# ScalarE in written order during the mLSTM outputs, own buffers for the decays' exponentials, and outputs that follow the states without a stop

## The chip, the cores and the metric

The kernel runs on one core of a Trainium2 chip. The metric is the device time of one execution in microseconds (us). Each engine of the core (TensorE for matmuls, VectorE, ScalarE, GpSimd, and SyncE, which here issues nearly all DMAs) works through its own list of instructions in the order that was fixed when the program was built, and waits on semaphores for the others. In the rows TensorE is PE (PEld its weight loads), VectorE is DVE, ScalarE is ACT, GpSimd is POOL, SyncE is SP.

## What is computed

Two layers of a hybrid backbone over 1024 latent tokens and 256 context tokens, width 1024. In each layer the tokens are normalised and modulated, and one input projection feeds three groups of heads:

```python
aq, ak, av, mq, mk, mv, mo, mg, pp = split(h @ w_in)
att  = softmax attention of 8 query heads on 2 key/value heads (aq, ak normalised and rotated)
ml   = bidirectional chunkwise mLSTM of (mq, mk, mv), gates from mg, read out through sigmoid(mo)
pool = centred means of pp over windows 2, 4, 8, 16, times a small matrix per group
x = x + g1 * (concat(att, ml, pool) @ w_out)
x = x + g2 * swiglu(norm(x))
```

The mLSTM of one direction runs over chunks of 128 tokens, for four heads of 64:

```python
b = cumsum(lf);  dmat = where(tril, b[:, None] - b[None, :] + li[None, :], -inf)
m_t = max(b + m, max(dmat));  w = exp(b + m - m_t)
s = (q @ k.T) * exp(dmat - m_t)              # the decays' exponentials
h = (w * (C @ q) + s @ v) / max(|den|, exp(-m_t))
C = a * C + v.T @ (wk * k)                   # the state, chunk after chunk
```

The second layer computes outputs for the latent tokens alone (8 chunks instead of 10).

## The kernel before

Python code writes the instructions of all engines in one sequence. A scheduler then fixes the order on each engine: it takes what is ready in its own estimate of times, the earlier written first, and gives out the buffers of each pool as it goes. An order that the code wants to keep is added as a dependency without a semaphore from one instruction to the next of the same engine; `InRow` (L87 to L105) does that for VectorE while a switch is on, and before the change that switch is on in one place, at the start of the feed-forward part (L1767 to L1794).

The in-projection of a layer runs TensorE as a row of GEMMs over one 128-column tile of `w_in` each (`gemm_tm` L796, `gemm_fm` L809), every one in blocks of 512 tokens (256 for the context), into PSUM banks of which this stage has 8. The work around the GEMMs is written as Python generators in the list `threads`; one call of `pump` lets every generator take one step. A block of 512 tokens gives two turns, one in the middle and one at its end, a block of 256 gives one. The step that a generator takes in a turn stands, in written order, between the halves of the GEMM or behind the block's eviction by ScalarE. `drain` takes turns until a generator, or all, have ended, with no GEMM between the turns.

- `ml_states` (L922) computes the states: 18 units of chunk and direction; a unit is a front (matmul `pk`, DVE `kw`, ACT and POOL `kh`) and a back (matmul `pu`, DVE `C`, snapshots into `X`, whose memory holds `qml`, `kml`, `vau` and `snap` in this stage). It takes 2 + 18 turns, and one in which it ends.
- `ml_outputs(z)` (L972) runs two generators, for the even and the odd chunks. One chunk (`ml_chunk`) takes 7 turns: 1 the loads of `sgc` and `mrow` (SP); 2 the matmuls `pst` and the first direction's decays; 3 the second direction's decays and `pxi`; 4 and 5 the numerators (matmul `pi`, eight DVE instructions each, then the square on ACT and its reduction); 6 the root; 7 the gains; and behind the seventh, in the turn of the next chunk's loads, `oh` (ACT, DVE) and its store to `mld`. In `decay_` (L996) a bank `pm` receives the exponents, ACT takes four exponentials into the tile `E`, DVE multiplies `E` by the scores, ACT rounds to `Ah`, POOL subtracts the rounding.
- `c_qk` and `c_q` (L1086, L1116) hold a query or key block in `q` and `sqq` for some four turns (ACT evicts, DVE and POOL rotate, ACT rounds, SP stores); a key block holds a third buffer `r`. `pool_tile` (L1182) forms the window sums on POOL in `bA`, `bB`, and uses `pm` and `ph`. `ada_fill` adds one small product for the layer's modulation per block, in the first layer only.

`E`, `q`, `sqq`, `r`, `pm`, `ph`, and in earlier parts of the stage `t`, `sq`, `vf`, `kw` and others, are all tiles of one pool of 2 KiB buffers, `f2k`, with 8 of them in this stage. Before the change `drain(stg)` stands behind the GEMM of `O_MQ + P`: the states that are left then run without a GEMM beside them, and the outputs are spawned behind them. Then come the GEMMs `O_PP`, `O_AK`, `O_AQ`, `O_PP + P`, three more `O_AQ`, `O_AV`, and a last `drain()`: 40 turns in the first layer, 34 in the second.

The attention stage follows in `phase("s")`: SP first issues the transposes of `mld` into `mixT[:, 4:6]` (the same memory as `h1`, which the last GEMM reads), the load of `pld`, and four loads `X <- xs` into the memory that the mLSTM used; then each of the 64 (first layer 68) units runs `Sp` (PE), its maximum `mx` (DVE), the exponential `pf` (ACT), `phl` (ACT, POOL), a transposing DMA `pT <- phl`, and `pv` (PE). The first filling matmuls of that stage (`pwo`) read `mixT[:, 4:8]`.

Of the kernel before, what the change touches and what calls it, by code (L numbers as in the profile page):

```python
# [9 lines left out]
F32 = mybir.dt.float32  # L10
# [8 lines left out]
P = 128  # L19
# [62 lines left out]
def hybrid_kernel(ctx: ExitStack, tc: tile.TileContext, I, out, dbg=None):  # L82
    nc = tc.nc
    order = mybir.DependencyInfo(mybir.DependencyClass.NoSync, mybir.DependencyReason.DATA)
    row = {"on": False, "last": None}

    class InRow:  # L87

        def __init__(self, e):
            self.e = e  # L90

        def __getattr__(self, name):
            f = getattr(self.e, name)

            def call(*a, **k):
                b = f(*a, **k)  # L96
                if row["on"]:
                    if row["last"] is not None:
                        tc.add_manual_dep(b.ins, row["last"].name, order, reason="written order")
                    row["last"] = b.ins  # L100
                return b
            return call

    def in_row(on):
        row.update(on=on, last=None)  # L105

    V = InRow(nc.vector)
    S, G, TE, DMA = nc.scalar, nc.gpsimd, nc.tensor, nc.sync
    MUL, ADD, SUB, MAX, MIN = ALU.mult, ALU.add, ALU.subtract, ALU.max, ALU.min
    dbg = dbg or {}  # L110

# [4 lines left out]


    cur = {}
    F2K = {"g": 8, "s": 6}
    PFB, PHB, PTB = 2, 3, 5  # L120

    def phase(kind):
# [29 lines left out]
    def pt_(shape, dt, tag, bufs=1, name=None):  # L152
        return cur["w"].tile(list(shape), dt, tag=tag, name=name or tag, bufs=bufs)

    def f2k(shape=(P, 512), dt=F32, name="f2k"):
        return pt_(shape, dt, "f2k", F2K[cur["kind"]], name)

# [44 lines left out]
    threads = []  # L202

    def spawn(gen):
        threads.append(gen)
        return gen
# [20 lines left out]
    def drain(g=None):  # L227
        while (g in threads) if g is not None else threads:
            if g is None:
                pump()  # L230
            else:
                try:
                    next(g)
                except StopIteration:
                    threads.remove(g)
# [531 lines left out]
    for l in range(DEPTH):  # L767
        last = l == DEPTH - 1
# [203 lines left out]
        def ml_outputs(z):  # L972
            for c in range(z, nto, 2):
                yield from ml_chunk(c, z)

        def ml_chunk(c, z):
# [19 lines left out]
            def decay_(d):  # L996
                pm = bank("pm")
                mm(pm.rearrange("p (h t) -> p h t", h=4), idb, mskb[:, d].unsqueeze(1).to_broadcast([P, 4, P]), start=True, stop=False)
                mm(pm, one3, mrow[d], start=False, stop=True)
                E = f2k((P, 4, P), F32, "E")  # L1000
                for i, h in enumerate(HO):
                    r = d * 64 + c * 4 + h
                    act(E[:, i], pm[:, i * P:(i + 1) * P], AF.Exp, bias=tmq[:, 0, r:r + 1])
                Ev = E.rearrange("p h t -> p (h t)")
                for g in range(2):
                    stt(Ev[:, g * 256:(g + 1) * 256], pst[g][:, 0:256], 1.0 / 16, Ev[:, g * 256:(g + 1) * 256], MUL, MUL)
                Ah = pt_((P, 2, 4, P), F16, "Ah", 4)
                act(Ah[:, 0].rearrange("p h t -> p (h t)"), Ev)
                tt(Ah[:, 1], E, Ah[:, 0], SUB, G)
                Ahs.append(Ah)  # L1010
# [137 lines left out]
        def q_roots():  # L1148

            v = rq[:, :, :nto].rearrange("p a c h -> p a (c h)")  # L1150
            rstd(v[:, 0], nto * 8, v[:, 2], v[:, 1])
            V.tensor_scalar(v[:, 0], v[:, 1], 0.125 / 16, None, op0=MUL)
            V.tensor_scalar(v[:, 1], v[:, 1], -0.125 / 16, None, op0=MUL)
# [28 lines left out]
        def pool_tile(i, u):  # L1182
            S2, S4, S8, S16 = (1, 0), (1, 1), (2, 2), (4, 4)
            for (t0, n) in blks:
                ub = u[:, pcol(t0) - 8:pcol(t0) + n + 8]
                bA = pt_((P, 768), F32, "pb", 2, "bA")
                bB = pt_((P, 768), F32, "pb", 2, "bB")

                def win(o, s, sh, lo_, hi_, x):

                    tt(o[lo_:hi_, x:n + 16 - x], s[lo_:hi_, x - sh[0]:n + 16 - x - sh[0]],
                       s[lo_:hi_, x + sh[1]:n + 16 - x + sh[1]], ADD, G)

                if i == 0:
                    win(bA, ub, S2, 64, 128, 7)
                    win(bB, ub, S2, 0, 64, 8)
                    win(bB, bA, S4, 64, 128, 8)
                    fin = [bB, bB]
                else:
                    win(bA, ub, S2, 0, 128, 1)  # L1200
                    win(bB, bA, S4, 0, 128, 2)
                    yield
                    win(bA, bB, S8, 0, 128, 4)
                    win(bB, bA, S16, 64, 128, 8)
                    fin = [bA, bB]
                p = f2k((P, 512), F32, "pm")
                for g in range(2):
                    ps = slice(64 * g, 64 * g + 64)
                    f = fin[g][ps, 8:8 + n]
                    if t0 != 512:  # L1210
                        tt(f[:, 0:8], f[:, 0:8], edge[ps, i, 0:8], MUL, G)
                    if t0 != 0:
                        tt(f[:, n - 8:n], f[:, n - 8:n], edge[ps, i, 8:16], MUL, G)
                yield
                for g in ([0] if fin[0] is fin[1] else range(2)):
                    ps = slice(0, P) if fin[0] is fin[1] else slice(64 * g, 64 * g + 64)
                    stt(p[ps, :n], fin[g][ps, 8:8 + n], invw[ps, i:i + 1], ub[ps, 8:8 + n], MUL, SUB)
                yield
                pb = bank("ppool")
                mm(pb[:, :n], pw[:, i], p[:, :n], start=True, stop=True)  # L1220
                sc = ps16[:, l * 2 + i:l * 2 + i + 1]
                ph = f2k((P, 2, 512), F16, "ph")
                act(ph[:, 0, :n], pb[:, :n], scale=sc)
                stt(ph[:, 1, :n], pb[:, :n], sc, ph[:, 0, :n], MUL, SUB)
                DMA.dma_start(out=pld[:, i, :, t0:t0 + n], in_=ph[:, :, :n])
                yield
# [6 lines left out]
        for (t0, n) in BLOCKS:  # L1233
            if t0 in nx:
                drain(nx.pop(t0))
            for r in range(3):
                if t0 >= T and last and r == 2:
                    continue
                if l == 0 and t0 < T:
                    pb = pf0[r][t0 // 512]  # L1240
                else:
                    pb = bank("pfm")
# [42 lines left out]
        for i in range(2):  # L1285
            DMA.dma_start(out=cst[i], in_=I["t_cs"][:, i])
        gemm_fm(O_MQ + P, blks, c_ml(qml, 1, INV * 4))
        drain(stg)
        spawn(ml_outputs(0))
        spawn(ml_outputs(1))  # L1290
        def pool_gemm(i):
            u = pool_u()

# [15 lines left out]
        while next_is_ada() or pend:  # L1309
            ada_fill()  # L1310
        drain()
        q_roots()


# [449 lines left out]
        sg, Sg, Su = sgs[0], f0.pop("Sg"), f0.pop("Su")  # L1764
        f0.clear()
        act(sg[:, :NTq], Sg[:, :NTq], AF.Silu, scale=INV)
        in_row(True)  # L1767
        stt(sg[:, :NTq], Su[:, :NTq], 1.0 / SW, sg[:, :NTq], MUL, MUL)

        ho = h_ops()  # L1770
# [20 lines left out]
        for _ in ho:  # L1791
            pass
        drain()
        in_row(False)  # L1794
        for k in range(4):
            split2(h2[:, k, :, H1], scv[:, k], V)

# [270 lines left out]
```

## Time and profile before

| | us |
|---|---|
| median of 3 runs (2774.57 to 2776.82) | 2776.61 |
| profiled execution, its own time | 2780.47 |
| its span (first to last instruction) | 2778.7 |
| PE busy | 2564.7 (92%) |
| DVE busy | 1890.2 (68%) |
| ACT busy | 1387.1 (50%) |
| POOL busy | 1269.3 (46%) |

The profiled execution took 3.9 us longer than the median of the runs. A wait in the rows below stands in square brackets: how long the engine had been idle before the instruction, and which engine's instruction, on which tile, released it last. "x12" is a count of instructions that were merged into one line. The granted clock is the share of TensorE's full speed that the throttle gave; of its two levels, 1.2 and 2.4 GHz, the mean over a stretch is shown.

### The profile page before, as it was taken

The page shows a single profiled execution, that of the slowest core. Times are in us where ns is not written, and L with a number is a line of the kernel's source. Part 1 is how long each engine was busy: PE and PEld are TensorE (multiplying, and loading weights), DVE is VectorE, ACT ScalarE, POOL GpSimd, SP SyncE. Part 2 cuts the span into 40 slices and gives each one's busy share as a digit, 9 for nine tenths or more (in the row PEclk, how much of TensorE's full clock was granted, in tenths as well). Part 3 has the DMA queues.
Part 4 walks back from the last instruction along what each step waited for, and adds up shares of the span by engine and source line. Part 5 has one row for each costly group of instructions (what it writes and reads, how often), then busy time and mean ns, then how long its engine had stood idle before and what let it go on. Part 6 is the DMA issues. An engine that isn't in the chain of part 4 may idle for free. (4 is left out here: it accounts for less than half of the span.)

```text
span 2778.7 us, 53623 instructions
## 1 busy us (share of the span) xinstructions
PE 2564.7 (92%) x21403; PEld 1500.9 (54%) x21403; DVE 1890.2 (68%) x3233; ACT 1387.1 (50%) x2650; POOL 1269.3 (46%) x963
## 2 busy tenths in 40 slices
PE   7999989987899999999999998888878899999997
PEld 4875556655555555555554684455545344444444
DVE  5558867778766555656565557866777767667676
ACT  5345557766443434444344544466765444444453
POOL 1124446774334435444443213456763465555651
PEclk9999999999899999999999999999989899999999
DMA  9544489995132222223212222389993111111211
GB/s 301 144 123 113 126 203 184 190 177 121 57 92 81 87 84 84 86 82 92 61 46 78 69 55 57 115 185 182 191 174 102 46 53 54 62 61 54 61 53 76
DMA packets 631629, 296.21 MB, mean 107 GB/s; under 512 B 362888, under 2 KB 620756, under 8 KB 630868
## 3 DMA queue, kind: packets, MB, share of 16 engines
q1 hardware_dynamic: 631204, 292.73, 42.9%
q8 instruction: 167, 2.74, 0.4%
q14 instruction: 82, 0.67, 0.1%
q10 hardware_dynamic: 176, 0.07, 0.0%
HBM read 176.19 MB, written 20.87 MB: 71 GB/s over the span
## 5 line engine op out<-in xcount | busy, mean ns | idle before, releaser
L1960 PEld LDWEIGHTS <-hlp 128*128 128x128 f16 x5040 | 492.0, 98 | 602.7 <-issue 26.6
L1960 PE MATMUL Swb<-T,hlp 128*128 128x512 f16 x1920 | 445.6, 381 | 18.5 <-DVE sg L96 13.0
L195 POOL TENSOR_TENSOR phl<-pf,phl 128x1280 f16<-128x1280 f32 (+1 forms) x132 | 345.2, 2618 | 176.8 <-ACT phl L175 123.1
L96 DVE SCALAR_TENSOR_TENSOR hlp<-ws,hlp 128x512 f16<-128x512 f32 (+1 forms) x320 | 231.6, 732 | 112.0 <-ACT hlp L175 89.2
L175 ACT ACTIVATE hlp<-ws 128x512 f16<-128x512 f32 (+1 forms) x320 | 162.6, 518 | 210.7 <-PE Swb L1960 90.5
L175 ACT ACTIVATE pf<-Sp,mx,rq 128x1280 f32<-128x1280 f32 (+1 forms) x144 | 189.6, 1317 | 118.1 <-DVE mx L96 98.8
L96 DVE TENSOR_REDUCE mx<-Sp 128x1 f32<-128x1280 f32 (+1 forms) x132 | 195.0, 1477 | 63.4 <-PE Sp L1337 55.4
L1960 PE MATMUL Swb<-tq,hlp 128*128 128x512 f16 x960 | 223.4, 382 | 8.0 <-DVE hlp L96 4.6
L1960 PE MATMUL Swc<-T,hlp 128*128 128x512 f16 x960 | 227.2, 379 | 0.0
L1400 PE MATMUL pwo<-T,hl 128*128 128x512 f16 (+1 forms) x960 | 194.5, 354 | 34.0 <-DVE X L96 14.3
L492 PE MATMUL pfm<-T,hl 128*128 128x512 f16 (+1 forms) x1032 | 216.4, 363 | 4.2 <-ACT E L175 4.1
L1337 PE MATMUL Sp<-T 128*128 128x512 f16 (+1 forms) x800 | 169.3, 348 | 42.5 <-ACT pf L175 40.1
L96 DVE SCALAR_TENSOR_TENSOR hlp<-st,hlp 128x256 f16<-128x256 f32 (+1 forms) x201 | 149.0, 746 | 86.7 <-ACT hlp L175 73.8
L195 POOL TENSOR_TENSOR ws<-st 128x256 f32<-128x256 f32 (+1 forms) x97 | 104.4, 1083 | 170.1 <-DMA st<-in_w_ffn_down_dram 67.9
L175 ACT ACTIVATE T<-sg 128x512 f16<-128x512 f32 (+1 forms) x170 | 98.8, 599 | 165.0 <-POOL sg L195 96.3
L1972 PE MATMUL dx<-T,hlp 128*128 128x256 f16 x1440 | 177.3, 273 | 1.0 <-DVE hlp L96 1.0
L195 POOL TENSOR_TENSOR X<-X,T 128x512 f32<-128x512 f32 x80 | 114.1, 1427 | 139.8 <-DVE X L96 105.1
L1960 PE MATMUL Swa<-T,hlp 128*128 128x512 f16 x720 | 169.3, 380 | 0.0
L1972 PEld LDWEIGHTS <-hlp 128*128 128x128 f16 x1440 | 139.1, 100 | 33.1 <-issue 4.8
L1400 PEld LDWEIGHTS <-hl 128*128 128x128 f16 x960 | 97.7, 102 | 109.8 <-issue 40.8
L175 ACT ACTIVATE phl<-pf 128x1280 f16<-128x1280 f32 (+1 forms) x115 | 144.6, 1262 | 21.2 <-DMA pT<-phl 18.9
L195 POOL TENSOR_TENSOR sg<-sg,T 128x512 f32<-128x512 f32 x60 | 88.7, 1478 | 143.6 <-DVE T L96 143.2
(308 smaller groups left out, 4735.8 us busy)
## 6 DMA issues: line engine op xcount, KB each, us to landing
T<-in_w_ada_dram SPq DMA_DIRECT2D x48, 512.0 KB
rawa<-in_w_ada_dram SPq DMA_DIRECT2D x48, 512.0 KB
st<-in_w_in_dram SPq DMA_DIRECT2D x32, 512.0 KB
st<-in_w_out_dram SPq DMA_DIRECT2D x64, 256.0 KB
st<-in_w_ffn_gate_dram SPq DMA_DIRECT2D x32, 512.0 KB
st<-in_w_ffn_up_dram SPq DMA_DIRECT2D x30, 512.0 KB
st<-in_w_ffn_down_dram SPq DMA_DIRECT2D x30, 512.0 KB
xs<-X SPq DMA_DIRECT2D x4, 2048.0 KB
```

What stands on the lines that cost most here:

```text
L96: b = f(*a, **k)
L175: b = S.activation(o, i, f, **kw).ins
L195: (e or V).tensor_tensor(o, a, b, op=op)
L492: mm(o, w[:, a, k, :], h[:, k, b, t0:t0 + n], start=(k == 0 and j == 0), stop=(k == nk - 1 and j == 2))
L1337: mm(Sp[:, e * nk + b0:e * nk + b0 + m], ql, qkv[:, 4 + h // 4, a, k0 + b0:k0 + b0 + m], start=(a == 0), stop=(a == 1), skip_group_check=True)
L1400: mm(pb, w[:, a, k, :], mixT[:, k0 + k, b, t0:t0 + n], start=(k == 0 and j == 0), stop=(k == 3 and j == 2))
L1960: mm(o, w[:, a, k, :], B[:, b], start=(s in "172" and k == 0 and j == 0), stop=(k == kh(i) - 1 and j == 2), skip_group_check=True)
L1972: mm(dbank[i][:, r * 256:(r + 1) * 256], w[:, a, k, :], B[:, b], start=(first and k == 0 and j == 0), stop=(not first and k == kh(i) - 1 a ...
```

## The change

The order switch gets a name and exists for ScalarE too. It is turned on for ScalarE behind the GEMM of `O_MQ + P` and off behind the last `drain()` of the stage, in both layers. `E` no longer comes from `f2k` but from two buffers of its own; to make room, `f2k` has 7 buffers instead of 8 in this kind of stage (it is also the stage at the kernel's start, at the seam of the layers and at the end), and `bA`, `bB` shrink from 768 to the 528 columns that are used. `drain(stg)` goes: a small generator `outputs` waits in `threads` until the states have ended, and then spawns the two output generators, while the GEMMs go on.

```diff
-    row = {"on": False, "last": None}
+    rows = {}
     class InRow:
-        def __init__(self, e):
-            self.e = e
+        def __init__(self, e, name):
+            self.e, self.row = e, rows.setdefault(name, {"on": False, "last": None})
...
-    def in_row(on):
-        row.update(on=on, last=None)
-    V = InRow(nc.vector)
-    S, G, TE, DMA = nc.scalar, nc.gpsimd, nc.tensor, nc.sync
+    def in_row(on, *names):
+        for name in names:
+            rows[name].update(on=on, last=None)
+    V, S = InRow(nc.vector, "V"), InRow(nc.scalar, "S")
+    G, TE, DMA = nc.gpsimd, nc.tensor, nc.sync
...
-    F2K = {"g": 8, "s": 6}
+    F2K = {"g": 7, "s": 6}
+    INROW = ("S",)
...
-                E = f2k((P, 4, P), F32, "E")
+                E = pt_((P, 4, P), F32, "E", 2)
...
-                bA = pt_((P, 768), F32, "pb", 2, "bA")
-                bB = pt_((P, 768), F32, "pb", 2, "bB")
+                bA = pt_((P, 528), F32, "pb", 2, "bA")
+                bB = pt_((P, 528), F32, "pb", 2, "bB")
...
         gemm_fm(O_MQ + P, blks, c_ml(qml, 1, INV * 4))
-        drain(stg)
-        spawn(ml_outputs(0))
-        spawn(ml_outputs(1))
+        in_row(True, *INROW)
+
+        def outputs():
+            while stg in threads:
+                yield
+            spawn(ml_outputs(0))
+            spawn(ml_outputs(1))
+
+        spawn(outputs())
...
         drain()
+        in_row(False, *INROW)
         q_roots()
...
-        in_row(True)
+        in_row(True, "V")
...
-        in_row(False)
+        in_row(False, "V")
```

## Rows read from the trace of the kernel before

**Rows 1.** The busy time of each engine in the two stretches from the states' last units to the end of the in-projection (first layer, second layer): start and end, length, busy us (instructions) of PE, PEld, DVE, ACT and POOL, mean granted clock, DMA share, GB/s.

```profile
188.00:373.00 185.00, 176.23 (x1866) 109.92 (x1859) 148.15 (x422) 95.22 (x250) 72.13 (x77) 0.97 0.43 123
1657.00:1821.00 164.00, 145.89 (x1328) 81.49 (x1326) 131.20 (x351) 78.83 (x194) 61.82 (x60) 0.93 0.30 88
```

**Rows 2.** The same view for the two attention stages.

```profile
383.00:653.00 270.00, 234.23 (x2886) 155.80 (x2885) 197.47 (x248) 194.54 (x270) 186.12 (x82) 0.97 1.04 187
1829.00:2091.00 262.00, 214.28 (x2580) 136.58 (x2580) 186.20 (x217) 183.30 (x231) 179.13 (x75) 0.93 0.99 182
```

**Rows 3.** What PE waited for in the second layer's stretch: us in total, times, the longest.

```profile
PE pfm L492 <- ACT E L175: 4.1, 1, 4.1
PE pxi L1024 <- ACT E L175: 4.1, 3, 2.0
PE msq L1091 <- ACT sqq L175: 1.9, 1, 1.9
PE pm L998 <- ACT u L175: 1.1, 1, 1.1
```

**Rows 4.** The same in the first layer's stretch.

```profile
PE pm L998 <- DVE num L96: 2.0, 1, 2.0
PE pxi L1024 <- DVE prm L96: 1.6, 1, 1.6
PE ppool L1220 <- DVE dn L96: 1.2, 1, 1.2
```

**Rows 5.** PE in order of time where the states run out: the second layer, with one unit beside the GEMM ahead of it (first three rows), and the first layer (last two).

```profile
1653.83 0.39 PE L931 MATMUL pk<-id,X 128*128 128x128 f16 x4
1654.14 0.39 PE L945 MATMUL pu<-X,kh 128*64 128x65 f16 x12
1654.46 2.76 PE L492 MATMUL pfm<-T,hl 128*128 128x512 f16 x12
1657.06 0.39 PE L931 MATMUL pk<-id,X 128*128 128x128 f16 x4
...
1667.05 7.05 PE L492 MATMUL pfm<-T,hl 128*128 128x512 f16 x22
188.24 0.40 PE L931 MATMUL pk<-id,X 128*128 128x128 f16 x4
...
193.36 4.92 PE L492 MATMUL pfm<-T,hl 128*128 128x512 f16 x22
```

**Rows 6.** ACT, and below it PE, in order of time around the longest wait of the second layer's stretch.

```profile
1703.51 0.48 ACT L175 ACTIVATE q<-pfm,qkg 128x256 f32<-128x256 f32 x1
1710.46 1.14 ACT L175 ACTIVATE E<-pm,tmq 128x128 f32<-128x128 f32 x4 [5.26 <-POOL q L195]
```

```profile
1676.20 2.76 PE L492 MATMUL pfm<-T,hl 128*128 128x512 f16 x12
1711.65 4.44 PE L492 MATMUL pfm<-T,hl 128*128 128x512 f16 x12 [4.09 <-ACT E L175]
```

**Rows 7.** ACT, and below it PE, in order of time in two later places of that stretch.

```profile
1742.52 0.42 ACT L175 ACTIVATE oh<-T 128x256 f16<-128x256 f32 x1 [3.39 <-DVE T L96]
1779.38 0.63 ACT L175 ACTIVATE sqq<-q 128x512 f16<-128x512 f32 x1 [2.06 <-DVE q L96]
```

```profile
1681.10 2.33 PE L492 MATMUL pfm<-T,hl 128*128 128x512 f16 x10
1750.13 4.31 PE L492 MATMUL pfm<-T,hl 128*128 128x512 f16 x12
1787.79 3.82 PE L492 MATMUL pfm<-T,hl 128*128 128x512 f16 x10
```

**Rows 8.** VectorE's busy time in the 20 us in which the second layer's last chunk pair gets its outputs, for the instructions on the tile `num`, then for those on `T` (here the memory of the outputs `hs`).

```profile
1792.00:1812.00 20.00, 6.03 (x20) 1.00 0.64 205
```

```profile
1792.00:1812.00 20.00, 5.59 (x14) 1.00 0.64 205
```

**Rows 9.** Two groups of these VectorE instructions: duration in ns as min/median/max, first and last start.

```profile
L96 DVE TENSOR_TENSOR dn<-num,tmq x4: 153/162/1224, 1792.6 to 1799.3; 128x4 f32<-128x4 f32 x4
...
L96 DVE TENSOR_TENSOR T<-num,dn x4: 408/422/426, 1795.0 to 1802.3; 128x256 f32<-128x256 f32 x4
```

**Rows 10.** SP in order of time at the seams to the attention stage: second layer, then first layer.

```profile
1805.79 0.59 SPq L1321 DMA_DIRECT2D X<-xs  x1
1809.40 2.69 SPq L1083 DMA_DIRECT2D mld<-oh  x4
...
1818.82 4.30 SPq L1317 DMA_TRANSPOSE T<-mld  x2
...
1829.46 12.62 SPq L1366 DMA_TRANSPOSE pT<-phl  x3
```

```profile
372.14 8.59 SPq L1317 DMA_TRANSPOSE T<-mld  x2
```

**Rows 11.** PE at the same seams: the first filling matmuls of the attention stage, first layer, then second.

```profile
382.87 1.44 PE L1400 MATMUL pwo<-T,hl 128*128 128x512 f16 x3 [3.39 <-DMA T<-mld]
```

```profile
1825.82 1.46 PE L1400 MATMUL pwo<-T,hl 128*128 128x512 f16 x6 [2.38 <-DMA T<-mld]
```

**Rows 12.** What PE waited for in the first 84 us of the kernel: us in total, times, the longest.

```profile
PE pf L723 <- POOL T L195: 2.4, 4, 1.2
```

More of the change, by code (lines that the diff above doesn't have):

```diff
@@ L84, in hybrid_kernel @@
     order = mybir.DependencyInfo(mybir.DependencyClass.NoSync, mybir.DependencyReason.DATA)
-    row = {"on": False, "last": None}
+    rows = {}
     class InRow:
-        def __init__(self, e):
-            self.e = e
+        def __init__(self, e, name):
+            self.e, self.row = e, rows.setdefault(name, {"on": False, "last": None})
         def __getattr__(self, name):
-            f = getattr(self.e, name)
+            f, row = getattr(self.e, name), self.row
             def call(*a, **k):
```

## The prediction

> **What bounds the kernel now.** I read the busy table of the page first (PE 92% of the span), then compared the two in-projection stretches that the change touches, each engine's sum in one row [rows 1]. The reader is to see that TensorE bounds both and yet stands still in them: in the first layer it is busy 176.2 of 185 us, in the second 145.9 of 164. So 8.8 and 18.1 us are idle, and the granted clock of 0.97 and 0.93 says that part of the busy time ran at the lower level. VectorE follows at 80%, ScalarE is near half. Nothing outside these stretches and their seams is edited but the buffer count, so idle PE time and the clock behind it are all that can be won here: at most some 27 us, and the matmuls that ran slow.
>
> Then I asked who ends these waits. In the second layer it is ScalarE: 4.1 us before a GEMM for `E`, 4.1 in three waits for `E`, 1.9 for `sqq`, 1.1 for `u` [rows 3]. In the first it is VectorE, which the change leaves in the scheduler's order [rows 4]. So the second layer has the gain.
>
> **No stop behind the states.** The second layer has used 12 turns when the drain comes, so 10 of the 18 units are done and 8 run bare; the first has used 15, 5 are left. In the second layer the bare run lasts from 1657.06 to 1667.05, 10.0 us. A unit beside a GEMM costs PE 0.63 us (1653.83 to 1654.46), so eight need 5.0, and two matmuls of the next GEMM (24 less the 22 that follow) 0.45; the other 4.5 us are waits of the chain PE, VectorE, ScalarE, POOL. The 22 matmuls behind it take 7.05 us; the same 22 take 4.92 in the first layer: the clock fell to the lower level after that run, 2.1 us more [rows 5]. In the first layer, 188.24 to 193.36 is 5.1 us, of which 3.15 and 0.45 are work: 1.5. Together 8.1 us. The cover is the GEMM; units interleaved with one cost nothing but their 0.63 us of PE. POOL's `kh` and ScalarE's copies move with them, past `u`; POOL has nothing else queued there.
>
> **Own buffers for `E`.** The longest wait: ScalarE evicts the third key block at 1703.5, then stands 5.26 us before the exponentials, until POOL's last product on `q` gives back a buffer; TensorE stands 4.09 us behind it, and its next twelve matmuls take 4.44 us instead of 2.76 [rows 6]. 4.09 + 1.68 = 5.8 us. With two own buffers this wait has no cause. What is late next is the second direction's `E`, which needs POOL's subtraction on the first; a turn lies between them.
>
> **ScalarE in written order.** The second layer's other ScalarE waits add to 7.1 us [rows 3], and two runs of slow matmuls follow such places: 4.31 against 2.76 for twelve, 3.82 against 2.33 for ten, 3.0 us [rows 6, 7]. In one of these places an earlier `sqq<-q`, waiting 2.06 us for VectorE, was put between two groups of exponentials [rows 7]; the outputs' generators are older than the queries' there, so written order has both groups first. In the other, `oh` waits 3.39 us for VectorE ahead of `E`, and written order has `oh` first too [rows 7]. Bounds: all 10.1 us won, or nothing won and as much again lost elsewhere, for each `Ah` now waits for VectorE's products before anything behind it (next `E`, evictions, banks) can go. One place of two is cured: I take half, 5.1 us.
>
> **The tail: what the change moves.** Outputs no longer start at turn 1. The states take 9 more turns in the second layer (8 units and the end), so the 29 turns of four chunks (4 x 7 + 1) lie in 10 to 38 of 34; in the first, 6, and 36 turns in 7 to 42 of 40. Before, they ended at 29 and 36. So the second layer's last chunk pair has its numerators, root, gains and `oh` behind the last GEMM, the first layer's its gains and `oh`. VectorE's work for a pair is 6.03 us on `num` and 5.59 on `T`, less four instructions of 0.42 in both: 9.9 us in the second layer [rows 8, 9]. In the first, six instructions on `T` of some 0.41 are left, 2.5. On VectorE the attention's first reductions queue behind these. On SP the stores to `mld` come first, then the transposes of `mld`, then `pT`; the reloads `X<-xs`, the last of which went at 1805.8, have to wait until the tail has read that memory. Before, the stores went 9.4 us ahead of the transposes [rows 10], and the filling matmuls were already held up by those transposes, 3.39 and 2.38 us [rows 11].
>
> Price: nothing, if the attention's start (its own chain leaves PE idle) covers it all; at most VectorE's 12.4 plus the transposes' own issue time, 8.6 and 4.3 [rows 10], if `pT` starts that much later: 25.3. I take VectorE's 12.4, since the reductions' place behind it is plain, while SP has slack of some microseconds ahead of the first `pT`.
>
> **Seven buffers instead of eight.** Waits for them have no row of their own. Near: POOL-released waits in the first 84 us, 2.4 [rows 12]. Between nothing (a later slot can even be the better one) and 2.4; I take 0.5, as `E` frees more than one buffer where the demand is highest. The smaller `bA`, `bB` have the same columns in use: nothing.
>
> **Sum.** 8.1 + 5.8 + 5.1 - 12.4 - 0.5 = 6.1 us won. The profiled execution's 2780.5 becomes 2774.4; it stands 3.9 over the median of the runs, so I forecast 2770.5.
>
> **Rivals.** First, slower: *the tail decides*. The last outputs reach `mld` behind the last GEMM; their transposes, and the reloads of `X`, enter a stage whose 16 DMA engines are at 1.04 and 0.99 of their time [rows 2], so every `pT` comes later and the stage ends later by as much. At its full 25.3 us: 19.0 - 25.3 - 0.5 = -6.8, or 2783; it decides once the tail costs more than the 19.0. For it: the DMA share, and the fills that already wait. Against it: TensorE is busy 87% and 82% of the attention stage [rows 2], so a late start can be made up in part. The Trainium skill, DMA: Bandwidth & Descriptors, section Issuing engines are not separate DMA queues, says that all queues end on the same 16 engines and interleave; by that rule the moved reloads slow the transposes whoever issues them, and the time is this rival's. No row here shows the two side by side.
>
> Second, no change: *the buffers stay short*. Three key blocks hold `q` and `sqq` each, one of them `r`, the pooling one: eight, of seven. ScalarE then waits at an eviction, in written order with all behind it: the 5.8 us stay, 0.3 us won, 2776.3. That is also where the change would not do what it says.
>
> Third, also no change: *VectorE is what is late*. An instruction of 0.16 us takes 1.22 in the worst case of four [rows 9], and the first layer's waits all end on VectorE [rows 4]; ScalarE's order then cures nothing: 5.1 less, 1.0 won, 2775.6. The GPSIMD Engine Reference of the Trainium skill, section Specifications, says that GpSimd shares its SBUF interfaces with VectorE and contends with VectorE instructions of two SBUF inputs; this `dn` has two, and the trace agrees with its 1.22 against 0.16. By that rule the order of a third engine would not change these waits, and the time is this rival's.
>
> Fourth, more: *the tail is covered* by the attention's start: 18.5 won, 2758.
>
> **How the numbers follow.** Forecast 0.36 (2764 to 2777), the tail 0.25, the second and third together 0.21, the tail covered 0.14, others 0.04. A measurement of this kernel tells about 0.2%, 5.6 us, from no change. Faster by more: 0.30 of the forecast, 0.14, 0.02: 0.46. Within: 0.06 + 0.02 + 0.16 + 0.01 = 0.25. Slower: 0.23 + 0.04 + 0.02 = 0.29. The forecast's own bounds are 24.0 won (every ScalarE wait, no tail) and 13.8 lost (none of them, the full tail, 2.4 of buffers): 2753 to 2790. The range, 2754 to 2788, leaves out the ends.
>
> **What would show it.** In the profile after: units of `ml_states` between GEMM halves, with no run of slow matmuls behind; no wait of `E` on POOL's `q`; the ScalarE-ended waits of [rows 3] halved; `oh` and the stores to `mld` behind the last GEMM, by some 10 us in the second layer; the first filling matmul and first `pT` of the attention stage later by the tail's price, and its end as well, or not. Wrong I am if the stretch itself does not get shorter by some 19 us in sum, or if the attention stage starts late by much more or less than 12.

## The result, and the profile after

The changed kernel takes **2812.83 us** (median of four runs, 2809.46 to 2813.56) against 2775.6 of the kernel before (four runs, 2774.57 to 2776.82): a ratio of **1.0128, with a 95% interval of 1.0112 to 1.0143**. That is some 37 us slower, where 2770.5 was forecast and 2788 was the top of the range. The profiled execution took 2813.56 us, its span is 2811.8.

To see where the time went, I read the same places off both timelines (us from the span's start):

| place | before | after | later by |
|---|---|---|---|
| first layer, first `u` evicted (behind the states' stop) | 198.3 | 196.2 | -2.1 |
| first layer, last `q` evicted | 358.4 | 368.8 | 10.4 |
| first layer, first `Sp` / first `pf` of the attention | 373.4 / 376.7 | 396.1 / 409.5 | 22.7 / 32.8 |
| first layer, first `Swb` (feed-forward) | 756.5 | 784.1 | 27.6 |
| second layer, first `pk` (states begin) | 1621.7 | 1648.4 | 26.7 |
| second layer, first `u` | 1674.1 | 1690.4 | 16.3 |
| second layer, last `q` | 1806.0 | 1825.5 | 19.5 |
| second layer, first `Sp` / first `pf` | 1821.1 / 1824.4 | 1853.5 / 1864.1 | 32.4 / 39.7 |
| end | 2778.7 | 2811.8 | 33.1 |

So the stop behind the states is won as forecast (10.4 us from the second layer's first `pk` to its first `u`, some of it the states' own work moved behind), and everything from there to the attention's first `pf` loses more. Of what the first `pf` is late, 5.2 us in the first layer and 6.6 in the second are made up again behind it. Those two stretches, first `u` to first `pf`, as the view by windows has them (start and end, length, busy us of PE, PEld, DVE, ACT and POOL, the granted clock, DMA share, GB/s). Of the kernel before:

```profile
198.30:377.00 178.70, 168.68 (x1752) 105.63 (x1753) 144.07 (x403) 91.61 (x238) 69.43 (x73) 0.97 0.45 130
1674.10:1824.40 150.30, 133.63 (x1178) 75.15 (x1179) 122.22 (x321) 72.33 (x177) 56.98 (x53) 0.94 0.34 96
```

Of the kernel after:

```profile
196.20:409.50 213.30, 183.85 (x1809) 112.80 (x1809) 149.16 (x417) 93.23 (x245) 71.73 (x75) 0.90 0.40 116
1690.40:1864.10 173.70, 147.01 (x1282) 84.68 (x1280) 127.84 (x345) 76.81 (x189) 60.62 (x58) 0.88 0.29 87
```

TensorE's idle time goes from 10.0 to 29.5 us and from 16.7 to 26.7, and the granted clock falls from 0.97 and 0.94 to 0.90 and 0.88: PE's busy time grows by 15.2 and 13.4 us, though only some 57 and 104 matmuls, the states' short ones, moved in. ScalarE does the same work (91.6 and 93.2, 72.3 and 76.8 us). What is new is what it waits for. The waits view of ScalarE (waited for, us in total, times, longest), kernel before, first layer from 198 to 374, then the second from 1653 to 1823:

```profile
ACT T L175 <- DVE T L96: 14.3, 7, 6.9
ACT Ah L175 <- DVE E L96: 3.3, 6, 1.2
...
ACT T L175 <- DVE T L96: 19.2, 5, 10.2
ACT Ah L175 <- DVE E L96: 4.1, 5, 2.0
```

Kernel after, 196 to 400, then 1680 to 1856:

```profile
ACT T L96 <- DVE T L96: 27.7, 9, 7.1
ACT Ah L96 <- DVE E L96: 20.4, 19, 3.5
...
ACT T L96 <- DVE T L96: 25.4, 7, 8.4
ACT Ah L96 <- DVE E L96: 17.6, 16, 4.7
```

These are the two places where an output's ScalarE instruction needs VectorE's product: `Ah` (the half-precision copy of `E` times the scores) and the square of `T`. In the first layer and in the second they are 1.9 and 1.3 times as long as before for the square, 6.2 and 4.3 times for `Ah`. How such waits hang together is seen in the timeline of the second layer after, here ScalarE, then VectorE, then TensorE:

```profile
1738.06 1.12 ACT L96 ACTIVATE E<-pm,tmq 128x128 f32<-128x128 f32 x4
1743.85 0.63 ACT L96 ACTIVATE Ah<-E 128x512 f16<-128x512 f32 x1 [4.67 <-DVE E L96]
1744.39 1.12 ACT L96 ACTIVATE E<-pm,tmq 128x128 f32<-128x128 f32 x4
1747.06 0.63 ACT L96 ACTIVATE Ah<-E 128x512 f16<-128x512 f32 x1 [1.55 <-DVE E L96]
1747.60 0.67 ACT L96 ACTIVATE q<-pfm,qkg 128x512 f32<-128x512 f32 x1
...
1741.07 0.41 DVE L96 SCALAR_TENSOR_TENSOR E<-pst,E 128x256 f32<-128x256 f32 x1
1743.32 0.17 DVE L96 COPY rq<-msq 128x8 f32<-128x8 f32 x1 [1.84 <-PE msq L1126]
1743.40 0.41 DVE L96 SCALAR_TENSOR_TENSOR E<-pst,E 128x256 f32<-128x256 f32 x1
...
1731.59 0.38 PE L1000 MATMUL pm<-mskb,idb 128*128 128x512 bf16 x1 [1.90 <-ACT sqq L96]
...
1746.75 5.28 PE L494 MATMUL pfm<-T,hl 128*128 128x512 f16 x12 [0.70 <-DVE E L96]
```

`E` is ready at 1739.2; VectorE does half of the product, then stands 1.84 us for TensorE's `msq`, then does the other half; ScalarE stands 4.67 us at `Ah`, with the next `E`, the next `Ah` and the eviction of `q` behind it. Three engines wait for each other in turn, and the twelve matmuls that follow take 5.28 us instead of 2.76 [rows 6]. The wait at `Ah` alone does not explain these slow matmuls: TensorE stood only 0.70 us before them, and the clock had fallen earlier. The windows view of this place, in the columns from above:

```profile
1724.00:1732.00 8.00, 4.26 (x28) 1.76 (x24) 6.29 (x11) 3.06 (x6) 3.90 (x3) 1.00 0.41 108
1734.00:1752.00 18.00, 17.30 (x108) 8.66 (x107) 11.42 (x30) 7.92 (x20) 6.29 (x5) 0.50 0.17 45
```

Up to 1732 TensorE had stood twice, 1.84 us for VectorE's `sqq` and 1.90 for ScalarE's, which had itself stood 2.31 us for POOL's `q`; from 1734 to 1752 the granted clock is 0.50, the lower level.

Some of what the prediction wanted to see is there too: units of the states stand between GEMM halves with no slow matmuls behind, no `E` waits for POOL's `q`, and `oh` and the stores to `mld` come 10.2 us behind the last GEMM's eviction in the second layer (1858.6 against 1848.4). Two of its signs are not: the waits that ScalarE ends for TensorE in the second layer add to 7.9 us where [rows 3] has 11.2, which is not half, and the two stretches are 34.6 and 23.4 us longer where they were to be 19 shorter in sum.

### The profile page after: what moved, and what is told of

Read it like the earlier page. It is cut to its first block, busy times and chain, and to the rows that moved or that the text cites. A ratio compares the mean times of both kernels' runs of the same rounds, so it can differ in the third digit from the quotient of the medians.

```text
span 2811.8 us, 53624 instructions
## 1 busy us (share of the span) xinstructions
PE 2581.0 (92%) x21403; PEld 1514.7 (54%) x21403; DVE 1893.6 (67%) x3233; ACT 1385.7 (49%) x2650; POOL 1269.9 (45%) x963
## 5 line engine op out<-in xcount | busy, mean ns | idle before, releaser
L1969 PEld LDWEIGHTS <-hlp 128*128 128x128 f16 x5040 | 491.7, 98 | 601.0 <-issue 23.4
L494 PE MATMUL pfm<-T,hl 128*128 128x512 f16 (+1 forms) x1032 | 226.9, 375 | 11.5 <-DVE hl L96 5.1
L96 DVE SCALAR_TENSOR_TENSOR hlp<-st,hlp 128x256 f16<-128x256 f32 (+1 forms) x201 | 150.3, 753 | 85.9 <-ACT hlp L96 72.1
L499 PEld LDWEIGHTS <-T 128*128 128x128 f16 x2784 | 153.6, 102 | 3.2 <-issue 2.1
```

What stands on the lines that cost most here:

```text
L494: mm(o, w[:, a, k, :], h[:, k, b, t0:t0 + n], start=(k == 0 and j == 0), stop=(k == nk - 1 and j == 2))
L499: mm(o, h[:, k, b, t0:t0 + P], w[:, a, k, :], start=(k == 0 and j == 0), stop=(k == NK - 1 and j == 2))
L1969: mm(o, w[:, a, k, :], B[:, b], start=(s in "172" and k == 0 and j == 0), stop=(k == kh(i) - 1 and j == 2), skip_group_check=True)
```

## The experiments

My **theory** after the traces: the written order of ScalarE is the larger part of the loss. **Rivals**: the late outputs (the tail), and the buffers (seven shared ones). Each part of the change can be made alone. The ratios below are to the kernel before, run beside each on the same chip. Every run changes the scheduler's order on the other engines along with its part; none shows what a new order alone brings, so differences of a few us are weaker evidence than the large ones.

| run | parts in it | ratio (95%) |
|---|---|---|
| after | order, own buffers, late outputs | 1.0128 (1.0112 to 1.0143) |
| `order_only` | order | 1.0099 (1.0076 to 1.0122) |
| `own_only` | own buffers, seven shared | 1.0041 (1.0027 to 1.0055) |
| `late_only` | late outputs | 1.0043 (1.0023 to 1.0063) |
| `no_late` | order, own buffers | 1.0115 (1.0095 to 1.0134) |
| `no_order` | own buffers, late outputs | 1.0049 (1.0031 to 1.0067) |
| `own_eight` | own buffers, eight shared | 1.0022 (1.0012 to 1.0033) |
| `late_faster` | late outputs, faster | 1.0031 (1.0020 to 1.0042) |
| `order_free_ah` | order without `Ah` | 1.0091 (1.0075 to 1.0107) |
| `order_free_hl` | order without `hl` | 1.0057 (1.0041 to 1.0072) |
| `order_free_out` | order without the outputs | 1.0044 (1.0027 to 1.0061) |
| `order_free_both` | order without outputs and `hl` | 1.0005 (0.9994 to 1.0016) |
| `x_behind` | as `no_order`, reloads later | 1.0124 (1.0107 to 1.0141) |
| `two_a_turn` | none; states two a turn | 0.9982 (0.9973 to 0.9992) |
| `two_second` | none; the same, second layer only | 0.9980 (0.9970 to 0.9990) |

**Which part costs.** `no_order`, on the changed kernel:

```diff
-    INROW = ("S",)
+    INROW = ()
```

> The changed kernel with ScalarE left to the scheduler's order again; own buffers for E and late outputs stay. Theory W (the written order is what costs: after it ScalarE stood 20.4 and 17.6 us before Ah for VectorE's products in the two layers, against 3.3 and 4.1 before): those waits fall back to some 4 us a layer, the stretches get shorter by the states' run and E's wait, the tail is what is left of a price: 2765 to 2780 us. Theory T (the late outputs are what costs, by a tail that ends behind the last GEMM and holds up the attention stage in both layers): the waits before Ah may fall, but the attention's first pf still starts some 25 us late in the first layer: 2800 us or more. Theory N (seven buffers instead of eight are too few): no better than 2805.

`no_late`, on the changed kernel:

```diff
+        drain(stg)
         in_row(True, *INROW)
-        spawn(outputs())
+        spawn(ml_outputs(0))
+        spawn(ml_outputs(1))
```

> The changed kernel with the stop behind the states put back: the outputs are spawned there, as before the change; written order and own buffers for E stay. Theory W: ScalarE's waits before Ah stay near 20 us a layer, the stretch stays slow, only the seam to the attention stage is won: about 2795 to 2805 us. Theory T: the tail is gone and with it most of the loss; own buffers bring some 6 us: 2770 to 2778 us. Theory N: no better than 2800.

`own_only` is both edits together:

> The kernel before with the own buffers for E alone (seven shared buffers instead of eight, smaller bA and bB); no written order, stop behind the states kept. Theories W and T both: the 4.09 us wait and the 1.68 us of slow matmuls of rows 6 are won, 0.5 lost: about 2770 us, 2765 to 2776. Theory N: seven buffers are short all over the GEMM stages, 2785 us or more.

`order_only` is `no_late` with the buffers of before:

```diff
-    F2K = {"g": 7, "s": 6}
+    F2K = {"g": 8, "s": 6}
-                E = pt_((P, 4, P), F32, "E", 2)
+                E = f2k((P, 4, P), F32, "E")
```

> The kernel before with the written order of ScalarE alone; E in the shared eight buffers, stop behind the states kept. Theory W: the larger part of the loss is here, 2790 to 2810 us, with ScalarE's waits before Ah at 15 us or more a layer. Theory T: within 6 us of the kernel before, 2770 to 2782. My prediction's own term for this part was 5.1 us won.

Measured: 2790.45, 2809.01, 2787.51 and 2804.52 us, against 2775.33. The order alone loses 29 us, three quarters of it all; taking it out of the changed kernel gives 22 back; taking the late outputs out gives 4, which the intervals do not tell from nothing. The first theory holds for the order, though `no_order` stays above its range of 2765 to 2780, and with a surprise: `own_only`, which both theories had at a gain, loses 12. Most of the order's loss lies in the first layer: there first `u` to first `pf` takes 198.6 us in `order_only` (178.4 before), in the second layer 157.7 (150.3). The parts do not add (0.99 + 0.41 + 0.43 = 1.83% against 1.28%). That they make the same engines wait in the same places would explain it; no run shows it.

**Own buffers.** Where `E` stood 5.26 us for POOL's last product on `q` [rows 6], `own_only` has, on ScalarE and then on TensorE:

```profile
1712.77 0.38 ACT L96 ACTIVATE sqq<-pfm 128x256 f32<-128x256 f32 x1 [4.99 <-POOL q L197]
...
1713.21 2.07 PE L1093 MATMUL msq<-sqq,bd 128*128 128x512 f32 x2 [4.18 <-ACT sqq L96]
```

The same wait, at an eviction. `own_eight` gives the eighth buffer back, with room from the gates' tile `Gt`, which moves into one of the `sgc` buffers:

```diff
-    F2K = {"g": 7, "s": 6}
+    F2K = {"g": 8, "s": 6}
-        Gt = pt_([P, 2, R], F32, "Gt")
+        Gt = pt_((P, 256), F32, "sgc", 2, "Gt")[:, :2 * R].rearrange("p (g r) -> p g r", g=2)
```

> The run own_only with eight shared buffers beside the two own ones for E; the room comes from giving the gates' tile Gt one of the two sgc buffers, which are not in use yet when the gates are worked out. Theory N (in own_only ScalarE's 5.26 us at E came back as 4.99 us at sqq<-pfm, both ended by POOL's q: with seven shared buffers the eviction is what runs out): with the eighth buffer back that wait goes too, 2766 to 2774 us, and TensorE's wait of 4.18 us before msq is gone. Rival P (POOL's chain on q is itself on the path, whoever waits for it): another wait ended by POOL's q appears and the time stays at 2780 us or more.

Measured: 2781.41 against 2775.67 us, still 6 worse than before, and better than `own_only` by 0.19%, some 5 us, which is just clear of the noise of 0.18. The eighth buffer is worth its price in the second layer alone: first `u` to first `pf` takes 155.8 us in `own_only`, 150.0 in `own_eight`, 150.3 before; in the first layer 183.2, 183.0 and 178.4. And the wait for POOL's `q` is in `own_eight` too, now at a pooling tile:

```profile
1712.13 0.69 ACT L96 ACTIVATE ph<-ppool,ps 128x512 f16<-128x512 f32 x1 [3.20 <-POOL q L197]
```

Rival P holds: whoever asks for the next shared buffer stands until POOL is done; the own buffers only choose who. In the first layer they add a wait: POOL takes a pooling window ahead of its two products on `q` and the first `Ah` between them, and `sqq<-q` stands 3.37 us (238.81) where it stood 0.39 before. The two smaller steps later in that layer (1.6 and 1.0 us) I have not followed.

**Late outputs.** `late_only` is `no_order` with the buffers of before (`F2K`, `E` and the columns of `bA`, `bB`).

> The kernel before with the late outputs alone (no stop behind the states; the outputs start when the states have ended); E in the eight shared buffers, ScalarE in the scheduler's order. If the costs of the parts add up (no_order 15.1 us over before, own_only 12.2): about 3 us over before, 2774 to 2783 us, with the first pf of the attention stages some 10 us late after Sp in both layers and the stretch itself shorter by some 8 us in the second layer. My prediction's own terms for it were 8.1 won and 12.4 lost. Rival: the late outputs are costly by themselves and own buffers soften them: 2785 us or more.

Measured: 2786.08 against 2775.67 us, 10 slower. The way from the last `q` to the first `pf` takes 39.1 us in the second layer and 34.4 in the first, against 18.4 and 18.3 before; from the first `pk` to the last `q` it takes 166.7 and 218.7, against 184.3 and 223.0. So 17.6 and 4.3 us are won ahead, and 20.7 and 16.1 lost at the end. The end of the second layer by windows, before and then `late_only`:

```profile
1794.00:1824.40 30.40, 28.50 (x345) 22.17 (x343) 26.47 (x71) 10.32 (x25) 4.27 (x3) 1.00 0.69 194
```

```profile
1790.00:1834.10 44.10, 30.77 (x436) 24.41 (x434) 35.18 (x121) 17.10 (x49) 8.04 (x6) 0.85 0.52 172
```

Is it the tail as such, or that the outputs have fewer turns? `late_faster`, on `late_only`:

```diff
+        def faster(g):
+            n = 0
+            for _ in g:
+                n += 1
+                if n % 3 != 2:
+                    yield
-            spawn(ml_outputs(0))
+            spawn(faster(ml_outputs(0)))
```

> The run late_only with the outputs' generators going three steps in two turns, so that the 29 turns from turn 10 on take some 20 and end at 30 of 34 in the second layer, and the 36 end at some 31 of 40 in the first, where they ended before the change. Theory T (late outputs lose by the tail: in late_only the way from the last q to the first pf is 39.1 us in the second layer and 34.4 in the first, against 18.4 and 18.3 before, while the GEMMs ahead of it are 15 us earlier in the second and 4 in the first): the way falls to some 20 us in both and part of the gain ahead stays, 2768 to 2778 us. Rival: the gain ahead was only the outputs' work not yet done; denser outputs put it back as VectorE's waits, 2780 to 2790 us.

Measured: 2784.39 against 2775.19 us. The first layer's way from the first `u` to the first `pf` is 190.5 us here, 193.6 in `late_only` and 178.4 before; the second's 162.1, 163.7 and 150.3. The tail is gone: from the last `q` to the first `pf` it takes 19.2 and 18.0 us, as before the change. But from the first `pk` to the last `q` it now takes 230.8 and 186.2, against 218.7 and 166.7 in `late_only`. Theory T, that the tail alone is the price, falls: with the tail cut short the time is nearly the same. I read it so: the outputs' 29 and 36 turns need turns beside GEMMs; the change takes 9 and 6 from them, and it makes little difference whether the rest is packed or hangs over the end. That the missing turns are the cause is argued from these two runs; the states' units now stand beside the later GEMMs as well, and no run tells the two apart.

**The states without the stop, and without moving the outputs.** `two_a_turn`, on the kernel before:

```diff
+    rate = {"n": 1}
     def pump(n=1):
-        for _ in range(n):
+        for _ in range(n * rate["n"]):
...
         spawn(stg)
+        rate["n"] = 2
...
+        rate["n"] = 1
         drain(stg)
```

> The kernel before, with two units of the states at each turn from their start to the stop in place of one, so that they have ended by the stop and nothing runs bare there; the outputs start where they did, no tail is moved. Theory S (the bare run of units is 6.6 us in the second layer and 1.5 in the first, as the prediction has it, and the late outputs only lost it again elsewhere): 2765 to 2770 us, no run of bare units, no slow matmuls behind. Rival: two units at one place stall on their own chain of VectorE, ScalarE and POOL, and give it back inside the GEMMs on the mLSTM's gates: 2774 to 2785.

Measured: 2770.83 against 2775.67 us, faster than both kernels, by 0.18% of the one before (0.08 to 0.27). From the first `pk` to the first `u` it takes 45.9 us in the second layer (52.4 before) and 61.3 in the first (62.9): 6.5 and 1.6 won. `two_second` does it in the second layer alone (`rate["n"] = 1 + l`):

> The run two_a_turn with two units a turn in the second layer alone. In two_a_turn the first layer had won 2.8 us at the first u and stood 0.5 late at the first Sp and 3.0 late at the first Swb, the second layer then won some 8 us. Theory S2 (the first layer's small bare run is worth nothing): 2765 to 2770 us. Rival (the differences of a few us behind the first layer come and go with the schedule): 2770 to 2776.

Measured: 2769.67 against 2775.19 us (12 and 19 runs), not to be told from `two_a_turn`. Its states on TensorE, two units behind each GEMM half, with the last GEMM at full pace (the 22 matmuls of [rows 5] took 7.05 us, these 48 take 10.53):

```profile
1650.54 0.39 PE L933 MATMUL pk<-id,X 128*128 128x128 f16 x4
1650.85 0.39 PE L947 MATMUL pu<-X,kh 128*64 128x65 f16 x12
1651.17 0.40 PE L933 MATMUL pk<-id,X 128*128 128x128 f16 x4
1651.50 0.39 PE L947 MATMUL pu<-X,kh 128*64 128x65 f16 x12
1651.82 2.76 PE L494 MATMUL pfm<-T,hl 128*128 128x512 f16 x12
1654.51 0.58 PE L947 MATMUL pu<-X,kh 128*64 128x65 f16 x24
1655.02 10.53 PE L494 MATMUL pfm<-T,hl 128*128 128x512 f16 x48
```

**What in the row costs.** `order_free_ah`, on `order_only`, takes one kind of instruction out of the row:

```diff
-                act(Ah[:, 0].rearrange("p h t -> p (h t)"), Ev)
+                nc.scalar.activation(Ah[:, 0].rearrange("p h t -> p (h t)"), Ev, AF.Copy)
```

> The run order_only with one kind of instruction taken out of the row: the copies Ah<-E, two for each chunk, may be placed by the scheduler again; everything else on ScalarE stays in written order. Theory A (the row costs because ScalarE stands at Ah until VectorE has made its product on E, which itself waits behind VectorE's instructions for TensorE, and the evictions that TensorE needs stand behind it: 20.4 and 17.6 us of such waits in the changed kernel): most of order_only's 29 us is back, 2775 to 2788 us. Rival O (any fixed order here keeps ScalarE from taking what is ready; the waits move to T<-T, sqq and oh, which also wait for VectorE): 2795 us or more.

Measured: 2800.22 against 2775.19 us; theory A falls. The waits moved. ScalarE in the first layer, `order_only` and then `order_free_ah`:

```profile
ACT T L96 <- DVE T L96: 34.8, 9, 8.9
ACT Ah L96 <- DVE E L96: 14.7, 20, 2.4
```

```profile
ACT T L96 <- DVE T L96: 39.8, 9, 10.0
...
ACT Ah L1010 <- DVE E L96: 4.5, 7, 1.2
```

And TensorE's longest wait in `order_only`'s first layer is of another kind, by the waits view and by ScalarE's and TensorE's timeline:

```profile
PE pfm L494 <- ACT hl L96: 6.9, 2, 3.5
```

```profile
274.29 0.38 ACT L96 ACTIVATE sqq<-pfm 128x256 f32<-128x256 f32 x1 [3.03 <-DMA T<-sqq]
274.57 1.05 ACT L96 ACTIVATE hl<-st 128x1024 f16<-128x1024 f32 x1
...
275.67 1.04 PE L494 MATMUL pfm<-T,hl 128*128 128x512 f16 x2 [3.36 <-ACT hl L96]
```

`hl<-st` makes the next GEMM's weights; it needs nothing but a panel whose load was issued 31 us before (243.8), but in the row it stands behind an eviction that waits for a buffer. In the changed kernel TensorE's largest waits in this stretch of the first layer (196 to 400) are for weight panels too, for the half that VectorE makes behind ScalarE's; the kernel before and `no_order` have none for `hl` there:

```profile
PE pfm L494 <- DVE hl L96: 5.1, 3, 3.4
```

So three more runs, on `order_only`: `order_free_hl` switches the row off around one instruction, `order_free_out` around all of `ml_chunk`'s, `order_free_both` around both.

```diff
+        on = rows["S"]["on"]
+        rows["S"]["on"] = False
         act(hv[:, 0], sv, scale=SW)
+        rows["S"]["on"] = on
```

> The run order_only with the weights' split hl<-st, one instruction of ScalarE for each weight panel, taken out of the row; all else in written order. Theory H (in order_only TensorE's largest wait in the first layer is 6.9 us in two for ScalarE's hl, the panel of the next GEMM: hl stands in the row behind an eviction that waits 3.03 us for a shared buffer, and TensorE has nothing left to do): a large part of the first layer's 18 us is back, 2785 to 2795 us in all, and no wait of pfm for hl is left. Rival O (the evictions behind the outputs' instructions make TensorE wait one by one, hl is only the last in their line): 2798 to 2806 us.

> The run order_only with all ScalarE instructions of the outputs (E, Ah, T<-T, s, oh) taken out of the row; evictions, queries and keys, pooling and the weights' split stay in written order among themselves. Theory G (the outputs' instructions, each behind VectorE's product, are what the rest stands behind: some 54 and 65 us of ScalarE's waits before T, Ah and oh in the two layers of order_only): 2775 to 2785 us. Rival (the row costs among the evictions themselves too, by the buffers of sqq and by hl): 2788 to 2800 us.

> The run order_only with both taken out of the row: the outputs' instructions and hl<-st. If H and G are both part of the cause: 2772 to 2780 us, no further from the kernel before than a few us. If what is left in the row (evictions, queries, keys, pooling) still costs: 2785 us or more.

Measured: 2796.57, 2791.54 and 2781.65 us, against 2780.06 beside them, 4.5 more than the kernel before took in the other comparisons. With that taken off, the first and the third lie in the ranges of H and of both; `order_free_out` lies between G's and its rival's, as `hl` is still in its row. Of the order's 0.99%, `hl` alone gives back 0.42, the outputs 0.55 (each give or take 0.3), both together 0.94. The row of evictions, queries, keys and pooling that is left costs nothing that can be measured, and wins nothing.

**The seam.** In the changed kernel the attention's first reduction in the first layer stood 7.46 us, ended by the landing of the stores to `mld`. SP's queue, then VectorE:

```profile
395.78 0.55 SPq L1330 DMA_DIRECT2D X<-xs  x1
399.27 1.77 SPq L1085 DMA_DIRECT2D mld<-oh  x4
401.10 0.49 SPq L1330 DMA_DIRECT2D X<-xs  x1
...
407.51 1.49 DVE L96 TENSOR_REDUCE mx<-Sp 128x1 f32<-128x1280 f32 x1 [7.46 <-DMA mld<-oh]
```

`x_behind` puts the reloads behind the transposes, on `no_order`, where that wait is 3.17 us:

```diff
-            DMA.dma_start(out=X[:, m:m + 2, :NTq], in_=xs[:, m:m + 2, :NTq])
+            xr_ = DMA.dma_start(out=X[:, m:m + 2, :NTq], in_=xs[:, m:m + 2, :NTq]).ins
+            tc.add_manual_dep(xr_, tm_.name, order, reason="reloads behind the transposes")
```

> The run no_order with the reloads X<-xs put behind the transposes of mld on SP. Theory D (at the seam the first reduction mx waits for the stores to mld, whose buffers lie where the attention's tiles come to lie, and the stores wait in the DMA engines behind 1.3 MB reloads): first pf after first Sp in some 5 us instead of 9.1 in the first layer, less to be had in the second, 4 to 8 us faster than no_order: 2782 to 2787. Rival B (the same bytes go through the same 16 engines, so what is won at the stores is lost at the first pT, or X is late for the first pwo): 2788 to 2794.

Measured: 2811.25 against 2775.67 us, some 21 slower than `no_order`. Theory D falls as a cure: the first `pf` comes 8.3 us after the first `Sp` (9.1 in `no_order`), and the first `pv` waits 6.6 us for its `pT` behind the four reloads (2.1 in `no_order`); in the second layer such waits are 8.0 us in three. From first to last `Sp` it takes 8.6 and 11.9 us more in the two layers, of which these waits are a part; the rest was not followed. Rival B had the direction and too small a size. That the wait at `mx` is for memory that `oh` gives up rests on the releaser in the trace; it was not tried by itself.

## Why the prediction was wrong, by its steps

The sum had the order at 5.1 us won, the own buffers with their price at 5.3 won, the states and the tail together at 4.3 lost. Made alone, the three lose 29, 12 and 10.

**ScalarE in written order** is the step that failed most: 5.1 us won in the sum, 29 us lost in `order_only`. I read the waits of [rows 3, 7], found two places where the scheduler had put an instruction badly, and priced the row by those. I did not price what the row does everywhere else: ScalarE has waits of 10 us for VectorE's `T` before too, but there no wait of TensorE in [rows 3, 4] ends on them. The lower bound, "as much again lost", was taken from the size of the gain; the nearer row for it was the waits view of ScalarE itself. And the range did not even use it: its slow end, 13.8 lost, has the order at nothing; with 10.1 lost it would be 23.9, some 2800 us. The prediction also looked at the second layer alone and priced nothing in the first, where 20 of the 28 us lie that the two stretches of `order_only` are longer. And I named "next `E`, evictions, banks" as what stands behind `Ah`, but not `hl<-st`, which every panel issues and which is some 40% of the loss (0.42 of 0.99). That both are the cause of `order_only`'s loss, and the order of the evictions is not, is shown by `order_free_both`; in the changed kernel the order was only taken out whole, by `no_order`.

**Own buffers for `E`**, 5.8 won less 0.5: the wait of [rows 6] went, but its cause, a buffer held until POOL's last product, stayed. `own_eight` gains 1.6 us at that place (the offset to the kernel before goes from 1.66 to 0.08 us between the evictions of `q` on either side of it), since `ph` stands 3.20. So the 5.8 was mis-sized by its larger part, and the second rival was right about this place, though with a price of 0.3 it was far too mild: the missing eighth buffer costs some 5 us, not 0 to 2.4.

**No stop behind the states**, 6.6 and 1.5 us: right to a tenth, 6.5 and 1.6 in `two_a_turn`, which puts the units beside earlier GEMMs where the change has later ones. In the whole time 4.8 us are left in `two_a_turn` and 5.5 in `two_second`.

**The tail**, 12.4: direction right, size and reason not. `late_only` loses 10 us in all where the prediction's two terms for it gave 4.3 lost. The way to the first `pf` is 36.8 us longer in sum, above my bound of 25.3; but much of that is work that was only moved past the GEMMs (21.9 us shorter ahead of it), and `late_faster` shows that the overhang is not the price by itself. The first rival had the sign, for its own reason; nothing here tells whose queue issues the reloads apart, as SP issues them all, so the rule that it cites from the Trainium skill (DMA: Bandwidth & Descriptors, section Issuing engines are not separate DMA queues) is not settled either way.

**VectorE is what is late**, the third rival: half right. Its instructions are what ScalarE waits for; but the conclusion that ScalarE's order "cures nothing" stopped at nothing, where it loses. The `dn` of 1.22 us does lie beside POOL's product on `q` (1799.34 on VectorE, 1799.25 to 1800.54 on POOL), but whether VectorE and POOL hinder each other was not tried.

## What to carry to other kernels

Before an engine is put in written order, list everything that it issues in the stretch, the neighbours' work too (here the next GEMM's weights), and for each instruction what it waits for: in a row, each wait is paid by all that stand behind it, so an engine that is half idle, as ScalarE was here, may still hold up the one that bounds. A wait for a buffer is cured at whoever holds the buffer, not at whoever asks. And work that runs bare was here better moved to earlier turns than into the turns of what follows it: two units a turn kept the gain that the late outputs gave back.

## What I had not expected of the hardware

Four stores to `mld` were issued between 399.27 and 401.04, and the first reduction, which the trace has waiting for them, started at 407.51, 6.5 us behind the last, with reloads of 1.3 MB each (128 x 2 x 1280 x 4 bytes) issued shortly before and right after; in `x_behind`, with no reload near, the first reduction goes 1.3 us behind the last of them (391.95 to 393.26). And the granted clock cost more than I had it: in the stretches above it was 0.90 and 0.88 on the mean, with TensorE busy 86% and 85% of the time, where it was 0.97 and 0.94 before, with TensorE busy 94% and 89%.
